# Column-major projections with the high and low parts of the activations side by side in one 512-column product

## The chip, the cores and the metric

One core of a Trainium2 chip runs the whole program. The time is device microseconds (us) of that core, from one launch; the median of several executions is used. TensorE (PE) multiplies, VectorE (DVE) and ScalarE (ACT) do the element-wise work, GpSimd (POOL) does a little, and SyncE's queue (SP) issues nearly all transfers.

## The reference

A trunk of two layers over 256 tokens of width 1024, all in float32. Each layer has a token mixer with two branches and then a feed-forward part: dense in layer 0, eight experts (two per token) in layer 1.

```python
def hybrid_mixer(h, w_in, conv_w, ..., w_up_dn, w_up_sb, w_out):
    proj = h @ w_in
    dn_qkv, dn_z, dn_b, dn_a, sb_q, sb_k, sb_v, gates = jnp.split(proj, SPLIT_AT, axis=-1)
    dn_qkv = causal_depthwise_conv(dn_qkv, conv_w)
    ...
    y_dn = o.reshape(B, S, DN_V).astype(h.dtype) @ w_up_dn
    ...
    y_sb = o_sb.reshape(B, S, SB_W).astype(h.dtype) @ w_up_sb
    g_dn, g_sb = jnp.split(jax.nn.sigmoid(gates), N_BRANCH, axis=-1)
    return (g_dn * y_dn + g_sb * y_sb) @ w_out

def swiglu(h, w1, w3, w2):
    return (jax.nn.silu(h @ w1) * (h @ w3)) @ w2
```

## The kernel before, in words

A float32 product is made of three products in TensorE's faster 32-bit type: weights and activations are each split into a high part (the value rounded to that type) and a low part (what the rounding left), and high x high, high x low and low x high are summed in PSUM.

The helper `gemm_t` (lines 368 to 388) makes the column-major projections: the output columns lie on the partitions and the 256 tokens along the free axis. It takes a 1 MB slab of weights, 256 output columns wide, in two blocks of 128 columns. `split` (lines 341 to 346) makes the high part of one block's weights on ScalarE (line 344) and the low part on VectorE (line 345), 1024 elements a partition each. Then TensorE runs 24 products of 256 columns for the block: eight of high weights with high activations (line 380), eight of high weights with low activations (line 382), eight of low weights with high activations (line 384). The two blocks of a slab fill the two halves of one PSUM bank of the tag "g", and then the caller's `each` reads the whole bank of 512 columns in one go. `w_up_sb` is the same with four products in place of eight.

Callers of `gemm_t`: in each mixer, four slabs each for q, k, v (through `conv`, which copies the bank with line 624, scales it twice from PSUM with line 627 and adds three shifted terms per half on VectorE, line 632), four for z (line 708, Silu), two for the query and two for the key of the second branch (lines 716 and 720), four for each gate (lines 883 and 891), two wide ones for `w_up_sb` (line 898), four for `w_up_dn` (`on_dn`, lines 1020 to 1027); in the dense feed-forward, 14 for w1 (line 1086, Silu) and 14 for w3 (line 1093). That is 72 blocks of 128 columns in each mixer (eight of them of the shorter kind) and 56 in the dense part. `narrow` (line 503) is a small product of the same kind, run once in each mixer. `gemm_n` (line 390) is the row-major projection (line 402 to 406): the activations are the stationary operand.

The program runs in four phases: mixer 0, dense feed-forward, mixer 1, experts. In the mixers the tag "g" has two banks, in the dense part three; the tile "t2" has six and four buffers. `hl`, the split weights, has three buffers in the mixers and six in the dense part. The high and low activations are two tiles of the tag "r8".

The mixer's order of issue is written as generators: the first slabs of k and z are drained, and then `fill` takes pieces of the other projections between the steps of the triangular inverse (`inverse`, products of 32x32 on line 767) and of the recurrence over the four chunks (lines 939 to 1004). A planner orders the instructions of each engine ahead of the run by readiness and program order; on the chip each engine works through its own list in that order. Between the pieces VectorE also works on the modulation vectors of a later layer (`ada_unit`, line 212, and `partial`, lines 220 and 221).

Of the kernel before, what the change touches and what calls it, by code (L numbers as in the profile page):

```python
# [19 lines left out]
P = 128  # L20
# [53 lines left out]
def trunk_kernel(  # L74
# [14 lines left out]
    phase_m = dict(r8=4, r4=2, f8=7, f4=6, t2=6, i2=5, s2=4)  # L89
    banks_m = dict(g=2, s=2, a=3, v=1)  # L90
    phase_f = dict(raw2=3, hl2=3, r8=2, f4=4, t2=4, t2r=4)
# [142 lines left out]
    def ada_first(l, mods):  # L234

        cs = mk("r4", [P, 4 * S])[:, : 32 * KC].rearrange("p (k c) -> p k c", c=32)
# [131 lines left out]
    def gemm_t(src, kc, n, act, each, rv=None):  # L368

        xh, xl = act  # L370
        if rv is None:
            rv = load(src.rearrange("(k p) n -> p k n", p=P), kc, n)
        for b0 in range(n // 256):
            ps = bank("g")
            pv = ps.rearrange("p (b t) -> p b t", t=S)
            for b in range(2):
                cb = 2 * b0 + b
                hv, lv = split(rv[:, :, cb * P : (cb + 1) * P], kc, P)
                for k in range(kc):
                    T.matmul(pv[:, b, :], hv[:, k, :], xh[:, k, :], start=(k == 0), stop=False)  # L380
                for k in range(kc):
                    T.matmul(pv[:, b, :], hv[:, k, :], xl[:, k, :], start=False, stop=False)  # L382
                for k in range(kc):
                    T.matmul(pv[:, b, :], lv[:, k, :], xh[:, k, :], start=False, stop=(k == kc - 1))  # L384
                if b == 0:
                    yield
            each(b0, pv)
            yield

    def gemm_n(src, act, each):  # L390

        xh, xl = act
# [4 lines left out]
        for b in range(2):  # L397
            w = slice(b * P, (b + 1) * P)
            for q, (hv, lv) in enumerate(parts):
                for i in range(4):  # L400
                    k = 4 * q + i
                    T.matmul(pv[:, b, :], xh[:, k, w], hv[:, i, :], start=(k == 0), stop=False)
                    T.matmul(pv[:, b, :], xl[:, k, w], hv[:, i, :], start=False, stop=False)
                for i in range(4):
                    k = 4 * q + i
                    T.matmul(pv[:, b, :], xh[:, k, w], lv[:, i, :], start=False, stop=(k == KC - 1))
# [56 lines left out]
    def normed(l, first, xn, banks="aaaa"):  # L463
# [3 lines left out]
        hh = mk("r8", [P, KC, S], F32R)  # L467
        hl = mk("r8", [P, KC, S], F32R)
# [9 lines left out]
        return hh, hl  # L478
# [24 lines left out]
    def narrow(wv, n, act):  # L503

        ps = bank("a")
        for i, part in enumerate(act):
            for k in range(KC):
                T.matmul(ps[:, 0:S], wv[:, k, :], part[:, k, :], start=(i == 0 and k == 0), stop=(i == 1 and k == KC - 1))
        t = mk("t2", [P, 512])
        A.copy(t[0 : 2 * n, 0:S], ps[0 : 2 * n, 0:S])  # L510
        ps = bank("a")
# [20 lines left out]
    def mixer(l, act, wba, router=None, ahead=None):  # L532
# [169 lines left out]
        def proj(base, u, each, rv=None):  # L702
            yield from gemm_t(
                wl[:, base + 256 * u : base + 256 * u + 256], KC, 256, act, lambda _, pv: each(u, pv), rv
            )
# [5 lines left out]
        def sq_unit(u):  # L711
            if u == 0:
                late["sqk"] = mk("f8", [P, 8, S])
            yield from proj(
                C_SQ, u,
                lambda u, pv: A.activation(late["sqk"][:, 2 * u : 2 * u + 2, :], pv, AF.Copy, scale=SBD**-0.5),
            )

        def sk_unit(u):
            yield from proj(C_SK, u, lambda u, pv: A.copy(late["sqk"][:, 4 + 2 * u : 6 + 2 * u, :], pv))  # L720
# [102 lines left out]
        oh = mk("r4", [P, 4, S], F32R)  # L823
        ol = mk("r4", [P, 4, S], F32R)
# [54 lines left out]
        def gs_unit(u):  # L879
            if u == 0:  # L880
                late["ms"] = mk("f8", [P, KC, S])
            yield from proj(
                C_GS, u, lambda u, pv: A.copy(late["ms"][:, 2 * u : 2 * u + 2, :], pv)
            )
# [807 lines left out]
```

## Time and profile before

| | us |
|---|---|
| median of three runs | 1948.24 (1946.54 to 1949.49) |
| the profiled execution | 1945.89 |
| its span | 1944.0 |
| PE busy | 1810.3 (93%) |
| PE weight loads busy | 1407.9 (72%) |
| DVE busy | 1598.7 (82%) |
| ACT busy | 1287.4 (66%) |
| chain that ended last, by engine | PE 64%, DVE 18%, ACT 7% |

The span is the time from the first to the last instruction. A busy share is an average over phases with different limits: the phases end at about 390, 627 and 990 us. PE products overlap one another, so the mean duration of one product is longer than the distance between two; the pace is read from the starts. The chain is followed back from the last instruction to whatever released each step.

### The profile page before, as it was taken

The numbers are of one execution on the slowest core, as the hardware profiler recorded it, in microseconds if no ns is written. First come the engines' busy times: TensorE is split into PE (matmuls) and PEld (weight loads), VectorE is DVE, ScalarE is ACT, GpSimd is POOL, SyncE is SP. The second block draws the span as 40 slices with busy tenths as digits, with TensorE's granted clock in tenths as the row PEclk, the third lists the DMA queues.
The fourth block names the chain that finished last, engine by engine and source line by source line (L and its number), as shares of the span: only waits on it lengthen the run. The fifth ranks groups of instructions, "written<-read, shape, count | busy, mean of one in ns | idle before, by whom it ended". The sixth has DMA issues, their size and how long they took to land.

```text
span 1944.0 us, 36722 instructions
## 1 busy us (share of the span) xinstructions
PE 1810.3 (93%) x14869; PEld 1407.9 (72%) x14869; DVE 1598.7 (82%) x1892; ACT 1287.4 (66%) x1842; POOL 72.6 (4%) x89
## 2 busy tenths in 40 slices
PE   7899999999999899999979998999889998899986
PEld 3789889999999789989968833687336863378522
DVE  4778688787666878588669899999989999998998
ACT  3755555444443665566468788878788787887885
POOL 0101000000000101000000001000010000000000
PEclk8999999999999999999989999999989999999998
DMA  8544446688773444455729999999999999999996
GB/s 304 169 154 133 158 153 222 218 300 280 244 258 100 131 156 132 153 173 190 277 99 393 368 406 344 406 384 366 386 341 412 375 373 373 371 406 372 382 397 238
DMA packets 219312, 539.27 MB, mean 277 GB/s; under 512 B 12570, under 2 KB 119524, under 8 KB 205028
## 3 DMA queue, kind: packets, MB, share of 16 engines
q1 hardware_dynamic: 215216, 536.02, 75.3%
q8 instruction: 150, 2.46, 0.5%
q10 hardware_dynamic: 3892, 0.35, 0.1%
q14 instruction: 54, 0.44, 0.1%
HBM read 535.27 MB, written 1.06 MB: 276 GB/s over the span
## 4 chain that ended last, share of the span: by engine, by line
PE 64%; DVE 18%; ACT 7%; issue 5%; DMA 4%; SPq 1%; ACTq 0%; DVEq 0%
PE g L1358 13%; PE g L380 7%; PE g L384 7%; PE g L382 7%; DVE lo L1279 6%; PE g L1378 5%; PE a L1447 5%; DMA raw<-in_moe_w_dram 3%; PE a L1452 2%; PE a L1462 2%; ACT hl L1275 2%; DVE t L632 2%; DVE hl L345 2%; PE a L1060 1%; PE a L1061 1%
## 5 line engine op out<-in xcount | busy, mean ns | idle before, releaser
L1279 DVE TENSOR_TENSOR lo<-raw,hl 128x2048 fp32r<-128x2048 f32 (+1 forms) x338 | 756.5, 2272 | 62.6 <-ACT hl L1275 60.3
L1275 ACT CAST hl<-raw 128x1024 fp32r<-128x1024 f32 x672 | 657.5, 1051 | 43.9 <-DMA raw<-in_moe_w_dram 25.7
L345 DVE TENSOR_TENSOR hl<-raw,hl 128x1024 fp32r<-128x1024 f32 (+1 forms) x252 | 298.0, 1188 | 137.2 <-ACT hl L344 136.6
L344 ACT CAST hl<-raw 128x1024 fp32r<-128x1024 f32 (+1 forms) x252 | 256.7, 1021 | 201.5 <-PE g L384 135.4
L380 PE MATMUL g<-r,hl 128*128 128x256 f32 x1536 | 235.2, 292 | 6.8 <-ACT r L488 3.4
L382 PE MATMUL g<-r,hl 128*128 128x256 f32 x1536 | 226.7, 287 | 0.0
L1358 PE MATMUL g<-hl,r 128*128 128x512 f32 x896 | 223.1, 391 | 1.9 <-ACT t L1333 1.2
L384 PE MATMUL g<-r,hl 128*128 128x256 f32 x1536 | 223.2, 286 | 0.6 <-DVE hl L345 0.6
L380 PEld LDWEIGHTS g<-r,hl 128*128 128x128 f32 x1536 | 204.0, 194 | 15.5 <-ACT r L488 4.7
L1378 PE MATMUL g<-raw,x 128*64 128x512 f32 (+1 forms) x1024 | 211.0, 558 | 0.0
L382 PEld LDWEIGHTS g<-r,hl 128*128 128x128 f32 x1536 | 203.0, 194 | 2.2 <-issue 1.8
L384 PEld LDWEIGHTS g<-r,hl 128*128 128x128 f32 x1536 | 202.0, 194 | 2.9 <-issue 2.0
L1358 PEld LDWEIGHTS g<-hl,r 128*128 128x128 f32 x896 | 167.2, 188 | 42.0 <-ACT hl L1275 5.2
L1378 PEld LDWEIGHTS g<-raw,x 128*64 128x64 f32 x1024 | 70.3, 140 | 110.8 <-issue 100.0
L1358 PE MATMUL g<-lo,r 128*128 128x512 f32 x448 | 120.9, 392 | 4.3 <-DVE lo L1279 4.3
L1462 PE MATMUL a<-raw,s 128*64 128x512 f32 x448 | 110.4, 635 | 0.0
L1358 PEld LDWEIGHTS g<-lo,r 128*128 128x128 f32 x448 | 83.5, 188 | 24.3 <-DVE lo L1279 7.2
L212 DVE SCALAR_TENSOR_TENSOR f<-raw,csil,f 128x1024 f32<-128x1024 f32 x70 | 92.6, 1322 | 6.3 <-DMA raw<-in_ada_w_dram 5.9
L1447 PE MATMUL a<-hl,t2r 128*128 128x512 f32 x224 | 89.4, 399 | 0.0
L1452 PE MATMUL a<-hl,t2r 128*128 128x512 f32 x224 | 87.5, 391 | 0.0
L1426 ACT CAST t2r<-a 128x512 fp32r<-128x512 f32 x56 | 32.7, 586 | 77.1 <-PE a L1422 77.0
L632 DVE SCALAR_TENSOR_TENSOR t<-t,conv,t 128x255 f32<-128x255 f32 (+2 forms) x144 | 61.8, 476 | 26.2 <-ACT t L627 26.1
(336 smaller groups left out, 2173.4 us busy)
## 6 DMA issues: line engine op xcount, KB each, us to landing
raw<-in_moe_w_dram SPq DMA_DIRECT2D x334, 1024.0 KB, 7.6
raw<-in_w_in_dram SPq DMA_DIRECT2D x60, 1024.0 KB, 5.5
raw<-in_ffn_w_dram SPq DMA_DIRECT2D x42, 1024.0 KB, 5.2
raw<-in_ada_w_dram SPq DMA_DIRECT2D x40, 1024.0 KB, 5.4
f<-in_ada_w_dram SPq DMA_DIRECT2D x8, 1024.0 KB, 11.9
raw<-in_w_up_dn_dram SPq DMA_DIRECT2D x8, 1024.0 KB, 5.0
raw<-in_w_out_dram SPq DMA_DIRECT2D x8, 1024.0 KB, 5.0
raw<-in_w_up_sb_dram SPq DMA_DIRECT2D x4, 1024.0 KB, 5.2
```

Source lines behind the costliest of these rows:

```text
L344: A.copy(hv, part)
L345: V.tensor_sub(lv, part, hv.bitcast(F32))
L380: T.matmul(pv[:, b, :], hv[:, k, :], xh[:, k, :], start=(k == 0), stop=False)
L382: T.matmul(pv[:, b, :], hv[:, k, :], xl[:, k, :], start=False, stop=False)
L384: T.matmul(pv[:, b, :], lv[:, k, :], xh[:, k, :], start=False, stop=(k == kc - 1))
L1275: A.copy(hi[:, h, :], raw[:, h, :])
L1279: V.tensor_sub(lo[:, h, :], raw[:, h, :], hi[:, h, :].bitcast(F32))
L1358: T.matmul(ps, x_[:, kk, :], w[:, k, 512 * b : 512 * b + 512], start=(kk == 0 and x_ is xh and w is hv), stop=(kk == KC - 1 and w is lv),)
L1378: T.matmul(banks[0][h, 0:half], x32[:, kk, :], w[:, k, half * i : half * i + half], start=(wide and kk == 0), stop=(kk == KC - 1), skip_gr ...
L1447: T.matmul(ye[nb], gh[:, gs], w[:, k, nw], start=(first and m == 0 and p == 0), stop=(last and m == n // 256 - 1 and p == 3),)
L1452: T.matmul(ye[nb], gl[:, gs], w[:, k, nw], start=False, stop=False)
L1462: T.matmul(ye[nb][h, :], g32[:, gs], w[:, k, 512 * nb : 512 * nb + 512], start=False, stop=(last and m == n // 256 - 1 and k == 1), skip_g ...
```

## The change

`gemm_t` puts the high and low activations next to each other (one tile of 2 x 256 columns for each k) and multiplies the high weights with both in one product of 512 columns. The first half of the bank then holds the terms with high activations, the second half those with low ones; the low weights go into the first slice of products of 256 columns as before (to the second half of the bank). So a block of 128 output columns takes a bank of its own; ScalarE copies its first half into an SBUF tile and VectorE adds the second half to it. The callers read that tile. In `conv` the copy of line 624 goes, since the tile is the copy; the copies of the second branch's query, key and of one gate go, since `gemm_t` writes their tile directly (the query's scale moves into an instruction of VectorE that was there already). `narrow` is changed in the same way. The tile tags change: `r16` (two, one in the dense part) and `r8` (one) in place of four `r8` and two `r4`, of the same size together.

```diff
-    def gemm_t(src, kc, n, act, each, rv=None):
-        xh, xl = act
+    def gemm_t(src, kc, n, act, each=None, rv=None, into=None):
...
+        both = act.rearrange("p k i t -> p k (i t)")
         for b0 in range(n // 256):
-            ps = bank("g")
-            pv = ps.rearrange("p (b t) -> p b t", t=S)
+            dst = None
             for b in range(2):
                 cb = 2 * b0 + b
+                ps = bank("g")
                 hv, lv = split(rv[:, :, cb * P : (cb + 1) * P], kc, P)
+                for k in range(kc - 1):
+                    T.matmul(ps, hv[:, k, :], both[:, k, :], start=(k == 0), stop=False)
                 for k in range(kc):
-                    T.matmul(pv[:, b, :], hv[:, k, :], xh[:, k, :], start=(k == 0), stop=False)
-                for k in range(kc):
-                    T.matmul(pv[:, b, :], hv[:, k, :], xl[:, k, :], start=False, stop=False)
-                for k in range(kc):
-                    T.matmul(pv[:, b, :], lv[:, k, :], xh[:, k, :], start=False, stop=(k == kc - 1))
+                    T.matmul(ps[:, S : 2 * S], lv[:, k, :], act[:, k, 0, :], start=False, stop=False)
+                T.matmul(ps, hv[:, kc - 1, :], both[:, kc - 1, :], start=False, stop=True)
+                if dst is None:
+                    dst = into(b0) if into else mk("t2", [P, 2, S])
+                A.copy(dst[:, b, :], ps[:, 0:S])
+                V.tensor_add(dst[:, b, :], dst[:, b, :], ps[:, S : 2 * S])
                 if b == 0:
                     yield
-            each(b0, pv)
+            if each:
+                each(b0, dst)
             yield
...
         def conv(pv, base, out):
-            src = mk("t2", [P, 2, S])
+            src = pv
             dst = mk("t2", [P, 2, S])
-            A.copy(src, pv)
...
-                lambda u, pv: A.activation(late["sqk"][:, 2 * u : 2 * u + 2, :], pv, AF.Copy, scale=SBD**-0.5),
+            yield from proj(C_SQ, u, into=lambda u: late["sqk"][:, 2 * u : 2 * u + 2, :])
...
-                        V.tensor_add(at, z, C["mask"])
+                        V.scalar_tensor_tensor(at, z, SBD**-0.5, C["mask"], ALU.mult, ALU.add)
...
-            drain([gemm_t(ffn_w1[j][:, w], KC, 256, act, lambda _, pv: A.activation(sl, pv, AF.Silu))])
+            drain([gemm_t(ffn_w1[j][:, w], KC, 256, act, lambda _, pv: A.activation(pv, pv, AF.Silu), into=lambda _: sl)])
```

## Rows read from the trace of the kernel before

**Rows 1.** Busy time of each engine by phase: stretch, length, engines, clock, DMA
```profile
34.00:390.00 356.00, 338.85 (x4526) 315.43 (x4527) 271.31 (x530) 210.20 (x396) 20.72 (x20) 0.97 0.53 172
390.00:627.00 237.00, 237.00 (x1682) 222.98 (x1682) 164.03 (x164) 100.69 (x116) 4.20 (x5) 1.00 0.72 242
627.00:990.00 363.00, 338.55 (x4568) 311.54 (x4566) 273.57 (x559) 208.94 (x402) 21.93 (x20) 0.99 0.50 165
990.00:1944.00 954.00, 875.79 (x4000) 551.86 (x3999) 880.83 (x613) 760.35 (x912) 22.58 (x32) 0.97 0.95 365
```
**Rows 2.** The chain that ended last by line, of the first three phases
```profile
by line: PE g L380 14.0%; PE g L382 12.9%; PE g L384 12.9%; DVE t L632 4.9%; DVE hl L345 3.8%; issue 3.3%; ACT hl L344 3.0%; DVE f L212 2.9%; PE a L767 2.6%; PE g L406 2.5%; PE g L402 2.4%; PE g L403 2.4%; DVE t L220 1.3%; PE v L648 1.2%; D
...
by line: PE g L382 22.9%; PE g L384 22.7%; PE g L380 22.3%; PE a L1060 10.3%; PE a L1061 10.2%; PE a L1062 10.2%; DVE x L1079 0.6%; DVE t L1078 0.6%; PE a L284 0.2%; PE a L229 0.2%; PE a L185 0.1%; issue 0.0%
...
by line: PE g L384 11.9%; PE g L380 11.4%; PE g L382 11.2%; DVE hl L345 5.3%; DVE t L632 4.4%; issue 4.0%; PE g L402 3.1%; PE a L767 2.9%; PE g L403 2.8%; PE g L406 2.8%; ACT hl L344 2.7%; DVE f L212 2.3%; DMA raw<-in_ada_w_dram 2.0%; ACT f
```
**Rows 3.** Timeline of PE in the dense phase: start, duration, instruction, count
```profile
457.48 0.40 PE L1060 MATMUL a<-hl,t2r 128*128 128x512 f32 x1
...
462.72 0.39 PE L1062 MATMUL a<-hl,t2r 128*128 128x512 f32 x1
462.95 1.12 PE L380 MATMUL g<-r,hl 128*128 128x256 f32 x8
463.90 1.12 PE L382 MATMUL g<-r,hl 128*128 128x256 f32 x8
464.86 1.12 PE L384 MATMUL g<-r,hl 128*128 128x256 f32 x8
465.82 1.12 PE L380 MATMUL g<-r,hl 128*128 128x256 f32 x8
```
**Rows 4.** Busy time by stretch inside the mixers, columns as in the first group
```profile
34.00:184.00 150.00, 140.10 (x2464) 129.25 (x2465) 119.21 (x261) 95.69 (x196) 11.32 (x9) 0.96 0.48 152
154.00:184.00 30.00, 28.77 (x632) 26.89 (x631) 28.66 (x68) 17.66 (x32) 6.28 (x6) 1.00 0.35 109
184.00:214.00 30.00, 29.68 (x580) 27.95 (x580) 14.74 (x22) 15.92 (x31) 2.50 (x4) 1.00 0.50 154
...
754.00:784.00 30.00, 28.34 (x624) 26.66 (x610) 28.99 (x67) 17.62 (x33) 7.19 (x7) 1.00 0.35 108
```
**Rows 5.** The same stretches, line 344 alone: ACT busy and its count of casts
```profile
34.00:184.00 150.00, 36.62 (x35) 0.96 0.48 152
...
214.00:244.00 30.00, 5.89 (x6) 1.00 0.55 183
627.00:784.00 157.00, 36.70 (x35) 1.00 0.44 137
```
**Rows 6.** The chain from 34 to 184 us: shares by line and number of pieces
```profile
by line: DVE t L632 10.1%; PE g L380 9.9%; PE g L382 9.1%; PE g L384 7.6%; DVE hl L345 7.2%; ACT hl L344 4.5%; issue 3.5%; PE a L767 3.3%; DVE f L212 3.3%; DVE f L753 2.5%; PE a L508 2.5%; ACT f L527 2.4%; DVE f L600 2.2%; DVE t L220 2.2%; 
308 pieces in order of time: start us, us, what
```
**Rows 7.** Instructions nearest to those added and removed: duration ns min/median/max, starts
```profile
L874 ACT CAST r<-s x8: 363/373/375, 265.5 to 911.5; 128x256 fp32r<-128x256 f32 x8
L875 DVE TENSOR_TENSOR r<-s,r x8: 414/418/426, 267.5 to 912.3; 128x256 fp32r<-128x256 f32 x8
L624 ACT COPY t<-g x24: 567/585/602, 46.8 to 819.5; 128x512 f32<-128x512 f32 x24
```
**Rows 8.** Timeline of DVE without a gap: start, duration, instruction
```profile
179.75 0.41 DVE L794 TENSOR_TENSOR i<-s,cst 128x256 f32<-128x256 f32 x1
180.09 0.14 DVE L324 SCALAR_TENSOR_TENSOR sm<-sm,sm 128x4 f32<-128x4 f32 x1
```
**Rows 9.** Waits of DVE, ACT, PE: us in total, times, longest
```profile
DVE t L1093 <- PE g L384: 7.8, 9, 2.8
...
DVE f L1022 <- PE g L384: 2.1, 4, 0.6
...
ACT hl L344 <- PE g L384: 43.0, 34, 3.0
...
PE g L380 <- ACT t L627: 1.4, 1, 1.4
```
**Rows 10.** Timeline at the end of `w_up_dn` in mixer 0, PE then DVE
```profile
350.32 1.12 PE L384 MATMUL g<-r,hl 128*128 128x256 f32 x8
...
351.48 0.69 DVE L1022 SCALAR_TENSOR_TENSOR f<-f,g 128x512 f32<-128x512 f32 x1 [0.52 <-PE g L384]
...
353.95 0.68 DVE L1025 SCALAR_TENSOR_TENSOR r<-f,r 128x512 fp32r<-128x512 f32 x1
```

More of the change, by code (lines that the diff above doesn't have):

```diff
@@ L505, in narrow @@
         ps = bank("a")
-        for i, part in enumerate(act):
-            for k in range(KC):
-                T.matmul(ps[:, 0:S], wv[:, k, :], part[:, k, :], start=(i == 0 and k == 0), stop=(i == 1 and k == KC - 1))
+        for k in range(KC):
+            T.matmul(ps, wv[:, k, :], act[:, k].rearrange("p i t -> p (i t)"), start=(k == 0), stop=(k == KC - 1))
         t = mk("t2", [P, 512])
         A.copy(t[0 : 2 * n, 0:S], ps[0 : 2 * n, 0:S])
+        V.tensor_add(t[0 : 2 * n, 0:S], t[0 : 2 * n, 0:S], ps[0 : 2 * n, S : 2 * S])
         ps = bank("a")
@@ L700, in mixer, with proj @@
         late = {}
-        def proj(base, u, each, rv=None):
+        def proj(base, u, each=None, rv=None, into=None):
             yield from gemm_t(
-                wl[:, base + 256 * u : base + 256 * u + 256], KC, 256, act, lambda _, pv: each(u, pv), rv
+                wl[:, base + 256 * u : base + 256 * u + 256], KC, 256, act,
+                each and (lambda _, pv: each(u, pv)), rv, into and (lambda _: into(u)),
             )
@@ L713, in sq_unit @@
                 late["sqk"] = mk("f8", [P, 8, S])
-            yield from proj(
-                C_SQ, u,
-                lambda u, pv: A.activation(late["sqk"][:, 2 * u : 2 * u + 2, :], pv, AF.Copy, scale=SBD**-0.5),
-            )
+            yield from proj(C_SQ, u, into=lambda u: late["sqk"][:, 2 * u : 2 * u + 2, :])
         def sk_unit(u):
-            yield from proj(C_SK, u, lambda u, pv: A.copy(late["sqk"][:, 4 + 2 * u : 6 + 2 * u, :], pv))
+            yield from proj(C_SK, u, into=lambda u: late["sqk"][:, 4 + 2 * u : 6 + 2 * u, :])
         def sv_unit(u):
@@ L820, in inverse @@
             yield
-        oh = mk("r4", [P, 4, S], F32R)
-        ol = mk("r4", [P, 4, S], F32R)
+        osb = mk("r8", [P, 4, 2, S], F32R)
+        oh, ol = osb[:, :, 0, :], osb[:, :, 1, :]
         def stick():
@@ L881, in gs_unit @@
                 late["ms"] = mk("f8", [P, KC, S])
-            yield from proj(
-                C_GS, u, lambda u, pv: A.copy(late["ms"][:, 2 * u : 2 * u + 2, :], pv)
-            )
+            yield from proj(C_GS, u, into=lambda u: late["ms"][:, 2 * u : 2 * u + 2, :])
             ada_tick()
@@ L898, in each @@
                 V.scalar_tensor_tensor(ms, ms, 1.0, pv, ALU.add, ALU.mult)
-            yield from gemm_t(w_up_sb[l][:, 512 * u : 512 * u + 512], 4, 512, (oh, ol), each)
+            yield from gemm_t(w_up_sb[l][:, 512 * u : 512 * u + 512], 4, 512, osb, each)
             ada_tick()
@@ L932, in mixer @@
         tap(f"hs{l}", hs)
[L935 to L936 removed]
+        odn = mk("r16", [P, H, 2, S], F32R)
+        th, tl = odn[:, :, 0, :], odn[:, :, 1, :]
         st = mk("f4", [P, H, P])
@@ L1027, in on_dn @@
                 )
-            drain([gemm_t(w_up_dn[l][:, 256 * u : 256 * u + 256], KC, 256, (th, tl), on_dn)])
+            drain([gemm_t(w_up_dn[l][:, 256 * u : 256 * u + 256], KC, 256, odn, on_dn)])
             ada_tick(int('0000'[u]))
```

29 lines of the change are left out of this document (13 added, 16 removed).

## The prediction, made before the changed kernel was run

> **What bounds the kernel now.** First the busy time by phase [rows 1]. The experts, from 990 us on, hold nothing that the change touches; the sum is made over the 956 us from 34 to 990. In the dense phase PE is busy for all of its 237 us, and no wait of PE is listed in it; in the two mixers PE is busy 339 of 356 and of 363 us, DVE 271 and 274. Next the chain that ended last [rows 2]. In the dense phase it runs on PE alone: the three lines of `gemm_t` make up 67.9% of it (161 us), the down product's lines 1060 to 1062 the rest. In the mixers these three lines carry 39.8% of 356 us (142 us) and 34.5% of 363 us (125 us); the rest of the path changes between DVE, ACT and other products. So some 428 us of the path are column-major projection, and only there is a faster product worth something.
>
> Then the mixers by stretch. Two kinds show. From 184 to 214 us DVE is busy for half the time and PE for nearly all [rows 4]; the chain's pieces there, and from 244 to 350, are mostly PE. From 34 to 184 us DVE is busy 119 of 150 us [rows 4], and the chain has more of DVE than of `gemm_t` [rows 6]: adding up its pieces by engine I get DVE 57, `gemm_t` 41, ACT 30 us. From 154 to 184 us, and at the same place in mixer 1, DVE is busy 28.7 and 29.0 of 30 us [rows 4]. I call 34 to 184 and 214 to 244, and in mixer 1 627 to 784 and 814 to 844, the mixed stretches: 367 us, in which the chain's pieces add up to DVE 144, ACT 71 and `gemm_t` 90 us.
>
> **What a wide product saves.** Between the products of 512 columns in the dense phase the distance is constant: 24 of them start from 457.48 to the next group's start at 462.95, 227.9 ns each. The 24 products of 256 columns behind them start from 462.95 to 465.82, 119.6 ns each [rows 3]. Two narrow products take 239.2 ns, one wide one 227.9: 11.3 ns saved a pair, since the columns stay the same and only a fixed part goes. A block of 128 output columns goes from 24 x 119.6 = 2.87 us to 8 x 227.9 + 8 x 119.6 = 2.78 us, 3.1%. That it takes one third fewer weight loads is worth no more: they run beside the products in both runs of the rows.
>
> On the path: dense phase 161 us x 3.1% = 5.1. In the stretches of the mixers where PE is the path, 88 us of `gemm_t` in each: 2.8 each, 5.5 together. In the mixed stretches 90 us: 2.8. Together 13.4 us to be gained if nothing is lost (all 1536 pairs, on or off the path, would be 17.4).
>
> The Trainium skill ("TensorE: Matmul & The Clock Gate", section "Back-to-back issue gap") puts the gap of an isolated product at 262 cycles for 256 columns and 518 for 512. By it a pair would save 6 cycles at 2.4 GHz, 2.5 ns, and the 13.4 us would be 3.0. The row above says 11.3 ns, and it decides.
>
> **What the change adds.** Each of 200 blocks (72, 72 and 56) gets a copy of 128x256 from PSUM on ACT and an addition of 128x256 with one operand in PSUM on DVE. Lines 874 and 875 are these very shapes: 373 and 418 ns [rows 7]. Where DVE works without a gap the next instruction starts 0.34 us after one of that size (179.75 to 180.09) [rows 8], so an addition takes 0.34 us of a full DVE; I take 0.30 for a copy on a full ACT by the same proportion, an estimate. What goes: a copy of 585 ns for each of 24 slabs of q, k and v [rows 7], and the whole-bank copies of query, key and one gate, 16 in all, of the same shape. So ACT gains little work for these, and about 0.6 us a slab for z, the other gate and the up products; DVE gains 200 x 0.34 = 68 us and loses nothing.
>
> In the dense phase DVE goes from 164 to about 183 of 237 us and ACT from 101 to about 118. Both stay under PE, and three banks leave two blocks' time (5.6 us) for a bank's emptying. The cover is PE's own work. I take nothing; if the cover fails the price is that of the bank's rival below.
>
> In the mixed stretches DVE is the path for 144 us. Casts of line 344 come there 41 in 180 us and 41 in 187 [rows 5]; the fourth stretch has six, as the second, so 0.22 a us: 144 x 0.22 = 32 additions fall where DVE is the path, 32 x 0.34 = 11 us. That is the upper end. The lower end is 2: DVE's idle time around them hides all but those of the two stretches that are already 96% full, where 7 additions each (2.4 us) meet some 1.2 us of idle time. I take 8, nearer the upper end because a block's addition frees its bank and can't be put off long. ACT: 71 us of path x 0.11 slabs a us x 0.3 us net = 2.5; 0 if hidden; I take 2.
>
> A chain that ends a phase part: the last block of `w_up_dn` ends on PE near 351.3, and `on_dn` ends at 354.6, while the row-major product is running on what is ready [rows 10]. The copy and the addition stand ahead of it now, 0.4 + 0.4 and two hand-overs, 0.9 us; the first block's halves are done under the second. 0 to 1.8 us for two layers; I take 1. The starts of the phases, where high and low parts now must both be there for the first product, I cost at nothing: the last low part was late before also, and 16 products of 24 stood behind it at most.
>
> The new waits: DVE's list is in order, so each addition holds back what is queued behind it (the low parts of `split`, conv's shifted terms, the `ada_unit` steps) until ACT's copy and, before it, PE are done. The nearest rows are line 1093, which waits for the same PE line, 7.8 us in 14 times, and line 1022 in the mixer, 2.1 in 4 [rows 9]: 0.5 us each. The upper end is 82 blocks in the mixed stretches x 0.5 us x 39% (DVE's share of the path) = 16 us. The lower end is below nothing by a little: the planner reorders DVE's and ACT's lists as a whole, and conv's bank is now free before its scalings rather than after them (the one wait of PE for line 627, 1.4 us) [rows 9]; -2. I take 3, as DVE has a fifth of its time idle in these stretches and the additions were placed by the planner when they should be ready.
>
> Sum: -13.4 + 8 + 2 + 1 + 3 = +0.6 us. The profiled execution took 1945.9, 2.3 less than the median of the three runs; on the median the forecast is 1948.8, and no difference that can be seen (a measurement of this kernel can tell about 0.2%, 3.9 us).
>
> **Rivals.** 1. *The additions are hidden.* DVE has 85 us idle in each mixer [rows 1], much of it waiting for casts, and if the additions slip into it, only the two full stretches pay: -13.4 + 2 + 1 - 1, about -11, 1937. For it: the dense phase's 5 us and the 5.5 us of the PE stretches are nearly sure. Against it: the chain's 144 us on DVE.
>
> 2. *The bank comes free late, and PE waits.* With two banks in the mixers a bank used to hold a pair of blocks (5.7 us until it was wanted again); now it is wanted 2.78 us after its block ends. The copy must wait for ACT (a cast of 1.05 us may be ahead) and the addition for DVE: 0.2 + 1.0 + 0.4 + 0.1 + 1.2 + 0.4 = 3.3 us in a bad case. It decides from the point where the addition ends over 2.78 us behind its block. Then PE waits 0.5 us: at each of 82 blocks of the mixed stretches, 41 us; at a third of them, 14 us. With the sum above this gives 1958 to 1963 and slower, with the in-order waits at their upper end beside it up to 1975. For it: casts already wait for PE's line 384 34 times in mixer 0 [rows 9], so cast and copy become ready together. Against it: only one wait of PE for line 627, the bank's reader, is there now.
>
> 3. *The wide product saves less than in the rows*, 2.5 ns a pair as the page's formula has it: the gain is 3.0 on the path and the additions stay, +11, 1959. The rows of one and the same stretch speak against it.
>
> That the change doesn't do what it says (the columns are not fewer, only the instructions) is in the first term already.
>
> **How the numbers follow.** The forecast, no difference, 0.36 (own range 1944.4 to 1952.1); rival 1, 0.30; rival 2, 0.31; rival 3, 0.03. Faster by over 0.2% 0.30, within 0.2% 0.36, slower 0.34. The range runs from 1935, the gain with all its covers, to 1964, the bank's wait at a third of the blocks; 0.1 is left out on each side, mostly the upper ends of several terms together.
>
> **What would show it.** In the profile after: wide products on one line 228 ns apart; the dense phase 5 us shorter with PE still without waits; the stretches from 184 to 214 and 244 to 350 us shorter by 1 to 2 us each; DVE's busy time some 80 us higher and fuller in the mixed stretches, the chain there with more of DVE. Rival 2 would show as waits of the first wide product for the new addition; rival 1 as a chain with no addition in it. The prediction is wrong if the dense phase doesn't shrink (the first term fails), or if the mixers move by more than 8 us either way.

## The result, and the profile after

The changed kernel took 1973.33 us (median of four runs, 1969.29 to 1979.52), the kernel before on the same chip 1948.87; the ratio is 1.0128, 95% interval 1.0109 to 1.0146. It is slower by 24.5 us, where the prediction said no difference (1948.8) and a range up to 1964. One execution of the run e1 below took 9758 us, five times all others, and is left out of every number.

In the changed kernel line 384 holds the first seven wide products of a block, 386 the eight narrow ones with low weights, 387 the last wide one, 390 the copy on ACT and 391 the addition on DVE. The page of the changed kernel: busy time of PE, weight loads, DVE and ACT, and the groups of the new instructions (the last two entries of a group are the idle time of the engine before it, and what ended it).

```profile
PE 1812.1 (92%) x13317; PEld 1327.5 (67%) x13317; DVE 1673.0 (85%) x2094; ACT 1331.1 (68%) x2004; POOL 68.8 (3%) x89
...
L384 PE MATMUL g<-r,hl 128*128 128x512 f32 x1336 | 371.4, 412 | 29.1 <-DVE t L391 15.9
...
L390 ACT COPY t<-g 128x256 f32<-128x256 f32 x168 | 61.8, 374 | 179.6 <-PE g L387 178.8
...
L391 DVE TENSOR_TENSOR t<-t,g 128x256 f32<-128x256 f32 x168 | 69.8, 416 | 32.5 <-ACT t L390 31.2
```

DVE gained 74 us and ACT 44 (for DVE 80 was forecast); each copy and addition takes what the rows of the same shape took [rows 7]. (168 of the 200 blocks are in these two groups; the others write a tile of another name.) New is that PE stands idle for 29.1 us before line 384.

Where the time is, by phase: busy time by stretch, from 34 us to the end of mixer 0, the dense phase and mixer 1, cut at the products that open the next phase (columns as in [rows 1]). Of the kernel before:

```profile
34.00:374.66 340.66, 326.65 (x4444) 304.58 (x4445) 257.32 (x492) 201.66 (x380) 20.41 (x19) 0.98 0.51 168
374.66:628.06 253.40, 250.27 (x1768) 234.73 (x1767) 179.05 (x202) 110.19 (x134) 4.52 (x6) 0.99 0.72 243
628.06:989.66 361.60, 337.18 (x4561) 310.32 (x4560) 272.25 (x554) 207.93 (x399) 21.93 (x20) 0.99 0.50 166
```

Of the changed kernel, and two stretches that answer to [rows 4]:

```profile
34.00:387.45 353.45, 326.73 (x3892) 272.79 (x3892) 286.25 (x569) 213.41 (x432) 19.36 (x19) 0.95 0.51 163
387.45:633.95 246.50, 243.30 (x1318) 209.80 (x1319) 197.97 (x256) 127.26 (x190) 3.85 (x6) 0.99 0.73 249
633.95:1011.55 377.60, 341.68 (x4009) 283.21 (x4007) 299.02 (x628) 222.61 (x453) 20.44 (x20) 0.96 0.49 159
...
154.00:184.00 30.00, 26.99 (x499) 22.33 (x498) 27.29 (x69) 13.12 (x24) 5.66 (x6) 0.89 0.36 107
184.00:214.00 30.00, 28.86 (x578) 23.97 (x579) 21.65 (x43) 16.03 (x33) 1.10 (x1) 1.00 0.47 142
```

The dense phase is 6.9 us shorter, the mixers are 12.8 and 16.0 longer; the experts are within 1.2. In the two mixers together PE's busy time went up by 4.6 us (663.8 to 668.4) and its idle time, stretch less busy, by 24.2 (38.4 to 62.6). The small rise of the busy time hides two movements: from stretches of 2 us, busy time times what the granted clock lacks of full, I estimate that PE lost 9.3 us to the lower clock in before's mixers and 24.1 in the changed kernel's. So 14.8 us more went into a slower clock, and the products themselves became about 10 us cheaper. By this estimate the loss of 28.8 us in the mixers is 24.2 of PE waiting and 14.8 of PE at the lower clock, less 10.

In the dense phase the first step of the prediction can be read as it stood. Timeline of PE there (start, duration, instruction, count):

```profile
472.21 1.75 PE L384 MATMUL g<-r,hl 128*128 128x512 f32 x7
473.80 1.12 PE L386 MATMUL g<-r,hl 128*128 128x256 f32 x8
474.75 0.40 PE L387 MATMUL g<-r,hl 128*128 128x512 f32 x1
474.98 1.77 PE L384 MATMUL g<-r,hl 128*128 128x512 f32 x7
...
477.77 1.77 PE L384 MATMUL g<-r,hl 128*128 128x512 f32 x7
```

Blocks start 2.77 and 2.79 us apart (2.78 forecast, 2.87 before), and seven wide products take 1.59 us to the next start, 227 ns each.

In the mixers it is different. Timeline of all engines about the first slabs of mixer 0 (the bracket is the idle time before the instruction, and what ended it):

```profile
48.09 0.39 PE L387 MATMUL g<-r,hl 128*128 128x512 f32 x1
...
58.61 0.63 PE L387 MATMUL g<-r,hl 128*128 128x512 f32 x1
58.78 1.04 ACT L613 ACTIVATE f<-f 128x1024 f32<-128x1024 f32 x1
...
60.35 1.28 ACT L614 ACT_TABLE_LOAD   x1
61.64 1.06 ACT L614 ACTIVATE f<-f 128x1024 f32<-128x1024 f32 x1
...
63.35 0.65 ACT L390 COPY t<-g 128x256 f32<-128x256 f32 x2
...
63.87 2.32 DVE L664 TENSOR_SCALAR sm<-sm 128x4 f32<-128x4 f32 x1
66.22 0.42 DVE L391 TENSOR_TENSOR t<-t,g 128x256 f32<-128x256 f32 x1
...
66.69 3.33 PE L384 MATMUL g<-r,hl 128*128 128x512 f32 x7 [6.77 <-DVE t L391]
...
67.76 0.41 DVE L391 TENSOR_TENSOR t<-t,g 128x256 f32<-128x256 f32 x1
...
71.06 1.77 PE L384 MATMUL g<-r,hl 128*128 128x512 f32 x7
```

One bank is full from 48.5 on (the block that ends with the first line), the other from 59.2, when PE finds none free for its next block. Both copies stand in ACT's list behind other work, at the end of it two activations of 128x1024 and a table load, and come at 63.35. The first addition stands in DVE's list behind line 664, which takes 2.32 us and itself waited for ACT, and ends at 66.6, 18.2 us behind its own block; the second ends at 68.2, 8.9 us behind its block. PE has stood idle for 6.77 us, and the seven products behind that take 3.33 us in place of 1.77. In before two banks held four blocks, and PE worked on at the same place:

```profile
58.99 1.12 PE L380 MATMUL g<-r,hl 128*128 128x256 f32 x8
...
62.30 1.12 PE L380 MATMUL g<-r,hl 128*128 128x256 f32 x8
...
66.76 1.22 PE L380 MATMUL g<-r,hl 128*128 128x256 f32 x8 [1.42 <-ACT t L627]
```

Waits of PE in the changed kernel, in mixer 0 and then in mixer 1: us in total, times, longest.

```profile
PE g L384 <- DVE t L391: 7.9, 3, 6.8
...
PE g L384 <- DVE sm L321: 2.4, 1, 2.4
...
PE g L384 <- DVE sm L323: 1.7, 2, 1.5
```

```profile
PE g L384 <- DVE t L391: 8.0, 3, 6.9
```

(In mixer 1 the other two are 2.4 and 1.7 again. Lines 321 and 323 are instructions of 0.16 us; in each of these waits an addition of line 391 ended beside them, just before PE went on, for example at 84.7 and PE at 84.87.) These waits of the first wide product are 12.0 and 12.1 us, where before had 1.4 in each mixer for line 627; the difference is most of PE's added idle time. That is rival 2, but as a few long waits and not as 0.5 us at many blocks, and with the clock beside it.

The additions themselves are little of the path. The chain by line from 34 to 184 us, which answers to [rows 6]:

```profile
by line: PE g L384 18.6%; DVE hl L345 8.9%; PE g L386 8.8%; DVE t L638 5.7%; ACT hl L344 4.5%; PE a L771 3.8%; DVE f L212 3.2%; issue 2.7%; DVE t L220 2.6%; DVE f L757 2.5%; PE a L514 2.2%; ACT s L788 2.2%; DVE t L391 2.2%; PE g L387 2.1%; 
```

Line 391 has 2.2%, 3.3 us; the products of `gemm_t` have 29.5% (44 us, 40 in before), at a slower clock.

### The profile page after: what moved, and what is told of

Read it like the earlier page. It is cut to its first block, busy times and chain, and to the rows that moved or that the text cites. A ratio compares the mean times of both kernels' runs of the same rounds, so it can differ in the third digit from the quotient of the medians.

```text
span 1967.1 us, 33912 instructions
## 1 busy us (share of the span) xinstructions
PE 1812.1 (92%) x13317; PEld 1327.5 (67%) x13317; DVE 1673.0 (85%) x2094; ACT 1331.1 (68%) x2004; POOL 68.8 (3%) x89
## 4 chain that ended last, share of the span: by engine, by line
PE 63%; DVE 18%; ACT 8%; DMA 5%; issue 4%; SPq 1%; ACTq 0%; DVEq 0%
PE g L1360 14%; PE g L384 12%; PE g L386 7%; DVE lo L1281 5%; PE g L1380 5%; PE a L1449 4%; DMA raw<-in_moe_w_dram 3%; PE a L1464 2%; DVE hl L345 2%; PE a L1454 2%; ACT hl L1277 2%; PE g L387 2%; ACT hl L344 1%; PE a L1424 1%; DVE f L212 1%
## 5 line engine op out<-in xcount | busy, mean ns | idle before, releaser
L384 PE MATMUL g<-r,hl 128*128 128x512 f32 x1336 | 371.4, 412 | 29.1 <-DVE t L391 15.9
L384 PEld LDWEIGHTS g<-r,hl 128*128 128x128 f32 x1336 | 250.5, 194 | 86.7 <-DVE t L391 18.6
L386 PEld LDWEIGHTS g<-r,hl 128*128 128x128 f32 x1536 | 215.2, 194 | 16.7 <-issue 0.3
L386 PE MATMUL g<-r,hl 128*128 128x256 f32 x1536 | 223.6, 287 | 0.1
L390 ACT COPY t<-g 128x256 f32<-128x256 f32 x168 | 61.8, 374 | 179.6 <-PE g L387 178.8
L391 DVE TENSOR_TENSOR t<-t,g 128x256 f32<-128x256 f32 x168 | 69.8, 416 | 32.5 <-ACT t L390 31.2
L387 PE MATMUL g<-r,hl 128*128 128x512 f32 x200 | 80.4, 402 | 0.0
```

Source lines behind the costliest of these rows:

```text
L384: T.matmul(ps, hv[:, k, :], both[:, k, :], start=(k == 0), stop=False)
L386: T.matmul(ps[:, S : 2 * S], lv[:, k, :], act[:, k, 0, :], start=False, stop=False)
L387: T.matmul(ps, hv[:, kc - 1, :], both[:, kc - 1, :], start=False, stop=True)
```

## The experiments

Medians, each beside the kernel before on the same chip. Of each edit only the lines that carry it are shown. A difference of two runs that each have an interval of 4 to 7 us about their distance from before is itself known to some 5 to 8 us; that holds for every term below that is got by subtracting.

| run | what differs | us | before | ratio, 95% interval |
|---|---|---|---|---|
| e1 | wide in the dense part alone | 1950.81 | 1949.53 | 0.9987 to 1.0027 |
| e9 | the same again | 1951.29 | 1951.13 | 0.9988 to 1.0022 |
| e2 | wide in the mixers alone | 1976.70 | 1949.53 | 1.0115 to 1.0188 |
| e3 | narrow, pair of blocks a bank, with copy and DVE step | 1972.45 | 1949.53 | 1.0082 to 1.0137 |
| e4 | change, products narrow | 1992.54 | 1949.53 | 1.0187 to 1.0242 |
| e8 | before, idle copy and DVE step | 1972.39 | 1951.13 | 1.008 to 1.016 |
| e11 | before, idle DVE step | 1962.86 | 1951.14 | 1.0031 to 1.0084 |
| e12 | before, idle ACT copy | 1961.26 | 1951.14 | 1.0033 to 1.0074 |
| e5 | change, four banks at the start | 1963.53 | 1951.46 | 1.0046 to 1.0098 |
| e6 | change, emptying ordered first | 1964.63 | 1951.46 | 1.0043 to 1.0091 |
| e7 | change, ACT empties both halves | 1971.46 | 1951.13 | 1.0082 to 1.0141 |
| e13 | change, four banks | 1955.65 | 1951.14 | 1.0011 to 1.0045 |
| e14 | e13, emptying first | 1961.48 | 1951.14 | 1.0029 to 1.0072 |
| e15 | before, four banks | 1961.40 | 1951.69 | 1.0024 to 1.0060 |
| e16 | e13, products narrow | 1971.71 | 1951.69 | 1.0075 to 1.0144 |
| e17 | wide in dense and late slabs | 1953.92 | 1951.69 | 0.9997 to 1.0028 |
| e18 | change, idle products in the stall | 1981.97 | 1951.69 | 1.0126 to 1.0194 |

**Which phase.** e1 and e9 are the same edit: `gemm_t` as before, and a wide copy of it for the dense part.

```diff
-    drain([gemm_t(ffn_w3[j][:, w], KC, 256, act, on3)])
+    drain([gemm_w(ffn_w3[j][:, w], KC, 256, act, on3)])
```

> Only the dense feed-forward uses the wide product with its copy and addition; both mixers are as before. Both theories give a gain here: PE is the path in all of that phase, three banks cover the emptying. From the row of the wide product (11.3 ns a pair) 5 us, from the phases of the changed kernel 7 us: 1942 to 1944. If the mixers' loss comes from somewhere else than the mixers' own blocks, the time would stay above 1949.

> The kernel with the wide product in the dense part alone, once more and in more rounds. In the first profile the dense phase was 6.4 us shorter, but mixer 1, with the same lists on every engine as before, took 4.0 us more, and the experts 3.4. If these two were scatter, the median comes out 4 to 7 us below the kernel before; if an earlier end of the dense phase is given back behind it, within 2 us of it.

The dense phase took 247.1 and 247.8 us in their profiles against 253.4 in before's, so the product gives there what it should. The whole did not get shorter: +1.3 and +0.2 us, and both intervals shut out a gain of 0.3%. In the profiles mixer 1 took 365.6 and 366.2 us, against 361.6 and 363.8 in two profiles of before, though the instructions of every engine there are in the same order. e10 is the kernel before once more, for the scatter of a phase.

> The kernel before, unchanged, with one more profile: how far the four phases of one and the same kernel differ between two executions. By the spread of its times (1946 to 1959) I expect the dense phase within 0.5 us, the mixers within 2 to 4, the experts within 4.

Its phases took 376.9, 253.0, 363.8 and 958.6 us: 2.2, -0.4, 2.2 and 4.3 off the first profile. So a phase can be read to some 4 us from one profile. Part of that is the start: line 475's first product comes at 20.58 us in the first profile of before and at 24.36 in this one.

In e1 and e9 most of the dense phase's gain is lost again at one place of mixer 1, the same in both (the two lines, of e1 and of e9):

```profile
693.11 0.32 PE L800 MATMUL a<-i,s 32*32 32x32 f32 x4 [3.02 <-issue]
...
696.12 0.32 PE L800 MATMUL a<-i,s 32*32 32x32 f32 x4 [3.01 <-issue]
```

In the middle of the inverse's small products (line 800, line 767 of before) PE stands idle for 3.0 us and waits for nothing that the profile shows, and its granted clock behind that is 0.50. Ahead of this place e1 is 6.9 us and e9 3.6 us earlier than before's first profile; behind it e1 is 2.0 earlier and e9 1.2 later. Neither profile of before has such a gap there (its longest of the kind is 0.7 us on that line). What causes it stays open; e3, e7, e8 and e13 to e17 have one to three such gaps of 1.4 to 3.8 us among these products too, the changed kernel and e4 have none; so a term that rests on one of those runs can be off by some 3 to 5 us for that reason alone.

e2 leaves the dense part as before (`gemm_o` is the old `gemm_t`) and changes the mixers.

```diff
-    drain([gemm_t(ffn_w3[j][:, w], KC, 256, act, on3)])
+    drain([gemm_o(ffn_w3[j][:, w], KC, 256, act, on3)])
```

> Only the mixers (and the narrow product) are changed, the dense part is as before. If the loss belongs to the mixers alone, 1948.9 + 12.8 + 16 = about 1978 to 1981, above the changed kernel. If it came from a coupling of the phases, it would be at or below 1973.

It took 27.2 us more than before, 1.3 below the expected range; mixer 0 ends at 387.9 us and mixer 1 takes 375.5, as in the changed kernel (387.5 and 377.6). The loss is theirs.

**Which part.** e3 has the added work with before's products and banks: narrow products, two blocks in a bank, then copy and a DVE step of the same shape for each (a maximum of the copy and the bank, which leaves the value as it is).

```diff
+    for b in range(2):
+        A.copy(dst[:, b, :], pv[:, b, :])
+        V.tensor_max(dst[:, b, :], dst[:, b, :], pv[:, b, :])
...
```

> Narrow products of 256 columns as before, two blocks in one bank as before; but the same copy of 256 on ScalarE and one instruction of 256 with a PSUM operand on VectorE for each block are kept (a maximum of the value with itself in place of the addition). Theory 'bank' (a block fills a bank, so two banks hold two blocks in place of four, and PE stalls until they are emptied): the added work by itself costs little, 1950 to 1958. Theory 'work' (the copies and additions lengthen ScalarE's and VectorE's path wherever they bound): the loss stays, and the gain of the wide product goes, 1975 to 1990.

e4 is the changed kernel with each wide product split into its two halves of 256 columns.

```diff
-    for k in range(kc - 1):
-        T.matmul(ps, hv[:, k, :], both[:, k, :], start=(k == 0), stop=False)
+    for i in range(2):
+        for k in range(kc):
+            T.matmul(ps[:, i * S : (i + 1) * S], hv[:, k, :], act[:, k, i, :],
...
```

> As the changed kernel, a bank for each block with its copy and addition, but each wide product is again two of 256 columns into the two halves. Both theories keep their loss; the difference to the changed kernel is what the wide product gains by itself: at most 17.4 us if every pair were on the path, 7 for the dense part alone: 1980 to 1990. At 1973 the wide product would be worth nothing, and the dense part's gain would have another cause.

Against before: e3 +22.9 (between the two theories, nearer to 'work'), e4 +43.0 (2.5 us above its range), the change +24.5. So copy and DVE step with before's banks cost 22.9, the bank for each block 20.1 more, and the wide product gives 18.5 back. The 22.9 are not the engines' time alone, since a bank is free only when the DVE step has read it. PE waits for that step in e3:

```profile
PE g L383 <- DVE t L393: 11.9, 6, 4.6
```

In before the waits for a bank's reader (line 627) are 2.8 us. e8 tests the work in another way: before, with an idle copy and an idle DVE instruction for each block, from SBUF to tiles that nobody reads.

```diff
+    some = rv[:, 0:2, cb * P : (cb + 1) * P]
+    A.copy(mk("ja", [P, 2, P]), some)
+    V.tensor_max(mk("jv", [P, 2, P]), some, some)
```

> The kernel before, with one more copy of 256 columns on ScalarE and one more instruction of 256 on VectorE for each block of the projections, from and to SBUF; nobody waits for them and they wait only for the loaded weights. Theory 'work': the same engine time as the change adds costs the same, 15 to 23 us, 1964 to 1972. Theory 'hand-over' (not the work costs, but that PE's bank is held and others' lists are held up by it): under 8 us, 1949 to 1957. The idle products' place: it changes no product and no bank.

+21.3, as e3. No bank and no product is touched here, so the added instructions cost that much without any hand-over of a bank. Busy time of e8's two mixers, columns as above:

```profile
34.00:384.09 350.09, 328.23 (x4445) 306.56 (x4446) 284.29 (x568) 227.84 (x457) 19.37 (x19) 0.97 0.51 163
638.49:1013.19 374.70, 343.08 (x4561) 315.05 (x4559) 295.68 (x626) 234.98 (x473) 20.39 (x20) 0.97 0.49 160
```

PE's idle time is 53.5 us there (38.4 and 42.1 in two profiles of before), its loss by the clock 17.6 as estimated above (9.3 and 9.6): 13 and 8 us, together the 21.3. But e8 is not the engines' time alone either. Its idle instructions wait for the weights, in lists that are worked through in order, and PE has more of the gaps in which it waits for nothing that the profile shows:

```profile
ACT ja L386 <- DMA raw<-in_w_in_dram: 35.5, 24, 4.2
...
DVE jv L387 <- DMA raw<-in_w_in_dram: 15.7, 13, 2.3
...
PE a L770 <- issue: 5.8, 6, 2.4
```

(In before, line 344 waits 4.4 us for one transfer of weights in all, and PE has 1.3 us of such gaps on that line.) The planner also put some 7% of the mixers' other instructions on DVE and ACT into another place of the order. How the 21.3 divide into work, these waits and the order is not shown.

e11 and e12 are e8 with one of its two instructions.

> The kernel before, with one idle VectorE instruction of 128x256 per block of `gemm_t` (a maximum of two weight tiles in SBUF, written to a tile that nobody reads); the products and the banks are those of before. The run with both idle instructions took 22 us more than before. Theory, VectorE's added time is what costs, since VectorE is on the path for 144 us of the mixed stretches: 15 to 22 us more than before (ratio 1.008 to 1.011). Rival, ScalarE's copies cost it: under 6 us more (below 1.003). If each carries about half, 9 to 13.

> The kernel before, with one idle ScalarE copy of 128x256 per block (from a weight tile in SBUF to a tile that nobody reads) and nothing else. Theory, VectorE costs: under 6 us more than before (ratio below 1.003). Rival, ScalarE's copies cost, because the casts that PE waits for stand behind them: 15 to 22 us more (1.008 to 1.011).

+11.7 and +10.1: neither theory, but half each (9 to 13 is what e11's text gives for that case), and their sum is e8's. DVE's term was sized about right (8, bound 11). ACT's was priced at 2, for the copies less those that go; e12 has all 200 copies and costs 10. Here too ACT stands 39.5 us in front of its idle copies, waiting for weights, so the 10 may be more than the copies themselves cost.

**Cures for the bank.** e7 takes DVE out of the emptying: ACT copies both halves and DVE adds later from SBUF.

```diff
+    low = mk("ja", [P, S])
     A.copy(dst[:, b, :], ps[:, 0:S])
-    V.tensor_add(dst[:, b, :], dst[:, b, :], ps[:, S : 2 * S])
+    A.copy(low, ps[:, S : 2 * S])
+    V.tensor_add(dst[:, b, :], dst[:, b, :], low)
```

> As the changed kernel, but ScalarE copies both halves of a block's bank (two copies of 256, the second into a tile of its own with three buffers), and VectorE adds the two later from SBUF. VectorE has as much to do as before, ScalarE some 0.3 us more a block (60 us in all), and a bank comes free without VectorE. Theory 'hand-over' (a bank is held until VectorE's list gets to its addition): the waits of the first wide product for the addition go, 8 to 15 us less than the changed kernel, 1958 to 1965. Theory 'work': 5 to 15 us more, 1978 to 1988.

1971.46, the change's time within the intervals, and in neither theory's range. PE's wait moves from DVE to ACT:

```profile
PE g L384 <- ACT ja L392: 11.8, 7, 3.3
```

e6 puts copy and addition ahead in the planner's order; e5 gives the first two slabs of k and of z four banks, tags g and s in turn.

```diff
+    with tc.high_priority(offset=300):
         A.copy(dst[:, b, :], ps[:, 0:S])
         V.tensor_add(dst[:, b, :], dst[:, b, :], ps[:, S : 2 * S])
```

> As the changed kernel, but the planner is told to put each block's copy and addition ahead of other ready work by 300 instructions of priority. Banks and work stay the same, only the order in ScalarE's and VectorE's lists changes. Theory 'bank': banks come free earlier, 5 to 12 us less, 1961 to 1968. Theory 'work': no change within 4 us, or slower where other work is the path.

```diff
-    ps = bank("g")
+    ps = bank(tags[b])
```

> As the changed kernel, but the first two slabs of k and of z in each mixer take their banks in turn from the tag g and from the tag s, which is idle then: four banks where the longest waits of the first wide product stand (6.8 and 2.4 us in each mixer, with TensorE at half clock behind them). Theory 'bank': these waits and the slow products behind them go, 10 to 18 us less than the changed kernel, 1955 to 1963. Theory 'work': no fewer instructions anywhere, so within 4 us of 1973.

Each gets about half of the loss back (+13.2 and +12.1); e6 lies in the range of 'bank', e5 0.5 us above it. e13 gives four banks to all slabs of k, z, q and v and to `w_up_dn`, e14 adds e6 to it.

> The changed kernel, but the two blocks of each slab of k, z, q, v and of the up product of the first branch take banks of the tags g and s in turn, so that four banks are in use in place of two. Theory, a bank per block costs some 20 us and four banks take that away: 1952 to 1962 (the run with four banks at the first two slabs alone took 1963.5). Rival, only the first slabs matter, or the banks of s are missed by the other products that use them: 1963 or more.

> The kernel of four banks, with the copy and the addition ahead of other ready work in the order of ScalarE and VectorE as well. Theory, a full bank stands between PE and its next block: each of the two cures took some 10 us alone; together 1948 to 1960. Rival, both take away the same stalls, or the work that is put back is then late: no better than the better of the two alone, 1962 to 1966.

e13 leaves +4.5, in the range of its theory. Its long stall in mixer 0 is still there, 6.11 us up to 72.68, but mixer 1 is 8.6 us shorter than the changed kernel's (369.0) and mixer 0 3.7; so of the 20 us between the medians the two profiles show 12.3 in the mixers. e14 is no better than e13 (+10.3): the rival comes nearest. That the work put back by the order is then late is not shown. e16 is e13 with narrow products.

> The changed kernel with four banks, each wide product split into its two narrow ones (the copy, the addition and the bank per block stay). What it takes more than the run with four banks (1955.65) is what the wide product gives where the banks are not short. Theory, the 11.3 ns of every pair and little more: 10 to 17 us more, 1966 to 1973. Rival, the 19 us between the narrow and the wide form at two banks were the product itself: 18 to 22 us more, 1974 to 1978. The other side: with four banks PE waits for other things and the product gives under 8 us.

1971.71, so the wide product gives 16.1 us with four banks (15.5 as both stand to before), in the range of the theory; and e16 lies 2.9 us below e3 as both stand to before, which is within the noise, so four banks take away about all that the bank for each block cost. e15 is the control: before with four banks.

> The kernel before, but its slabs of z and v, and every other slab of q and of the up product of the first branch, take a bank of the tag s in place of g: four banks in turn, two blocks in each as before. A control for the run with four banks: if the banks matter only because the change gives each block one of its own, before gains nothing from them. Theory: within 3 us of before. Rival, two banks were short before the change also: 4 to 10 us less than before.

Neither of the two: before gets slower, +9.7. Its wait for those banks is new, by other products that use the tag s (line 229, of the modulation vectors):

```profile
PE s L229 <- DVE cs L221: 13.4, 4, 6.4
```

So before gains nothing from four banks, but the control is not a clean one: these waits alone could make the 9.7 us. An edit of banks also moves the planner's order, and the gaps of 3 us in PE come and go with it; a single run's difference of some 5 us is not to be put down to its one edit.

**Where in the mixers.** e17 keeps k, z, q and v (64 of the mixers' 144 blocks) as before and makes the other 80 and the dense part wide.

> The change in the dense part, and in the mixers only for the query, key and gates of the second branch, the first branch's gate and the up products, where PE bounds the mixer; the slabs of k, z, q and v, whose work lies in the mixed stretches, are made as before (narrow products, two blocks in a bank, the copy in conv back). Theory, the loss sits in the slabs of k, z, q and v: within 4 us of before, 1945 to 1954. Rival, the added work costs wherever it lies: 1958 to 1966, about half of the change's loss.

+2.2, interval -0.6 to +5.5: most of the loss sits with the slabs of k, z, q and v, where DVE and ACT are wanted too. It is not shown that the other blocks are free: in e17's profile the mixers take 715.8 us, against 702.3 and 706.7 in the two of before (the change 731.1). Part of that is a gap of 3.8 us in PE at 105.9, which waits for nothing that the profile shows, and a later start (line 504's first product at 25.80). No run was faster than before.

**The clock.** Granted clock about the stall in the changed kernel (columns as in [rows 1]):

```profile
60.00:64.00 4.00, 0.00 (x0) 0.00 (x0) 1.53 (x3) 3.97 (x13) 1.22 (x1) 0.88 0.59 168
64.00:68.00 4.00, 1.31 (x3) 1.11 (x4) 3.97 (x5) 0.95 (x2) 3.20 (x3) 0.50 0.27 94
68.00:72.00 4.00, 4.00 (x19) 3.30 (x19) 3.93 (x11) 0.75 (x2) 0.00 (x0) 0.77 0.00 0
```

0.50 is the lower level, 1.2 GHz. e18 fills the stall with idle products: 50 of 128 columns ahead of the second slab of k in each mixer, into a bank that nobody reads.

```diff
+    if warm and b == 0:
+        keep_warm(warm)
     ps = bank("g")
...
```

> The changed kernel with 50 idle products of 128 columns in each mixer (into a bank that nobody reads) ahead of the first block of the second slab of k, where PE stood idle for 6.8 us and then worked at a granted clock of 0.50. Theory, the lower clock comes of the idle time in front of it: the seven wide products behind the stall take 1.8 us and not 3.3, the clock there is 1.00, and the two mixers together take 2 to 6 us less than in the changed kernel's profile. Rival, the clock falls there whatever PE did before: 3.3 us and 0.50 again, and a time as the changed kernel's, 1970 to 1976.

Timeline of PE in e18, and its granted clock there:

```profile
60.36 9.99 PE L453 MATMUL a<-ones,cst 128*128 128x128 f32 x88
70.10 1.87 PE L386 MATMUL g<-r,hl 128*128 128x512 f32 x7
```

```profile
64.00:68.00 4.00, 4.00 (x38) 4.00 (x38) 3.97 (x4) 1.55 (x4) 3.81 (x3) 1.00 0.48 167
68.00:72.00 4.00, 3.98 (x29) 3.32 (x27) 4.00 (x10) 0.00 (x0) 0.00 (x0) 1.00 0.02 4
```

The clock stays at 1.00 and the seven products take 1.87 us: it is the idle time that lowers it. The time did not go the expected way: +30.3 against before, where the change has +24.5 (the two intervals overlap). The trace has two records for each of the 50 products, and they ran for 11 us in place of the stall's 6.8. PE's idle time in the mixers fell by 8 us (62.6 to 54.6) and its loss by the clock from 24.1 to 16.1, and some 23 us of idle products more than ate that. The Trainium skill ("TensorE: Matmul & The Clock Gate", section "HAM oscillation — how this bites in real kernels") warns that gaps of PE between bursts put the clock back each time; the trace agrees, and by the estimate above the changed kernel loses 14.8 us more that way than before.

## Why the prediction was wrong, point by point

Two steps failed. The bank that each block now has to itself stood in no term of the sum and costs about 20 us. The added copies and additions were put at 10 us, 13 with the in-order waits, and cost 21 to 23. The saving of the wide product held.

*The wide product, -13.4: right.* The distance on the chip is the forecast's (227 ns, 2.78 us a block), and the dense phase fell by 6.9 where 5.1 was forecast. The runs give -18.5 at two banks (e4) and -16.1 at four (e16). That is nearer to the ceiling of 17.4 for all pairs than to the share on the path, but 13.4 lies within the noise of both. Rival 3 would have left 3.0; the runs speak against it.

*The added work, 8 + 2: this term failed.* e8 and e3 put it at 21 to 23, with all that comes with it. DVE's part is 11.7 (e11), at the upper end of its bounds. ACT's is 10.1 (e12) where 0 to 2.5 was forecast (the product that is written there, 71 x 0.11 x 0.3, is 2.3). The step that failed: ACT's copies were weighed only where ACT itself was in the chain (71 us), net of the copies that go. They cost more than that. That casts, which PE and DVE wait for, stand in ACT's list behind such a copy and are late by it is the likely way, but it was not tried by itself. (The copies that go in the change are still in e8 and e12, and their idle instructions wait for weights; so for the change itself ACT's part may be less. e3, where the copies are gone, is no lower, but has PE's waits for the bank in it.)

*The in-order waits, 3 (bounds -2 to 16).* They can't be told from the work. e3, in which the copies wait for PE and PE for the bank (11.9 us), and e8, in which the idle instructions wait for weights, cost the same to 2 us, but each with waits of its own; no run adds the work without any. (The nearest row was read as 7.8 us in 14 times; it has nine waits, in 14 slabs, of 0.9 us each.)

*The bank, costed at nothing; rival 2 had it.* e4 less e3 is 20.1 us. The rival's price was worked out from an addition that ends 3.3 us behind its block in a bad case. At PE's three longest waits in mixer 0 the trace shows 18.2 us (48.5 to 66.6), 7.4 (77.3 to 84.7) and 5.9 (164.0 to 169.9), since much more than one cast stood ahead in the two lists. The reason against it, that before shows only one wait for the bank, 1.4 us [rows 9], was no evidence: before's two banks held four blocks, the change's hold two. That three banks suffice in the dense phase was right: no wait for a bank is listed there, and a block's addition ends 0.85 us behind it (475.15 to 476.00).

*The clock, not costed at all.* Behind the idle gap of 6.8 us seven products take 3.33 us for 1.77. In the mixers the lower clock makes, by the estimate above, 14.8 of the 28.8 us lost. It is no further term of the sum: it is in the runs' prices of the work and of the bank, and is one reason why both are higher than rows of busy time gave.

*The end of a phase, 1.* No run took it alone.

With the measured terms the sum is -18.5 + 22.9 + 20.1 = 24.5; it closes because e3, e4 and the change are steps of one chain. What e8, e13 and e16 add is that terms of the same size come out by other ways: 21.3 (with waits of its own kind), about 20 and 16.1.

## What to carry to other kernels

A product with more columns saves a fixed part; if its result needs more PSUM and more work to empty it, as here, that has to be set against it. Count the blocks that the banks can hold when both emptying engines are late by the longest stretch of other work in their lists, and not by the usual cast. In a kernel like this one (PE 93%, DVE 82%, ACT 66% busy, each with a list in order) don't take added work on the less busy engine as hidden: 140 us of it on DVE and ACT cost 21, where shares of one chain gave 10. A run with idle instructions of that shape costs one line, but read its waits too, since they bring some of their own. The Trainium skill ("Perfetto Trace Analysis", section "Matmuls") asks both for larger products and for groups that rotate through PSUM banks; here the first took the second away, 16 to 18 us against 20.

## What the chip showed that was not expected

DVE's line 664, an instruction on 128x4 elements, took 2.32 us in the stall (the median of its eight is 171 ns); it lies beside POOL's line 619, which runs 62.78 to 66.16, and both end together. In before the same two stand side by side, 2.38 and 3.44 us. Whether the one holds the other was not tried. The Trainium skill ("SBUF — State Buffer", section "Who interferes with whom") says that GpSimd and some VectorE instructions take a pair of ports in turn, and that the later one waits until the earlier has ended; the times agree with that, and it would make some 2 us of the stall. In e13 the two stand side by side again, 2.31 and 3.38 us.

And a phase with the same order of instructions on every engine differs by 2 to 4 us between two profiles of one kernel, which is as much as most of the terms that the prediction weighed. With the dense part changed ahead of it (e1 and e9) the same order of instructions also got a gap of 3 us in PE that no wait in the profile explains.
